# Layer 0's entry: x tiles loaded and normed behind the context tiles' projection

## Chip, cores, metric

One core of a Trainium2 chip. The metric is the device time of one execution in microseconds (us). The engines are TensorE (PE: matmuls and transposes), VectorE (DVE), ScalarE (ACT), GpSimd (POOL) and SyncE (SP, which here issues nearly all DMA transfers). Each runs its own instructions in the order in which they were put on its queue; across engines they wait for each other by semaphores.

## The reference

A two-layer backbone: 512 latent tokens `x` and 256 context tokens `ctx`, width 1024. Each layer makes a modulation (shift, scale, gate) from a conditioning vector, one for x tokens and one for context tokens, and applies it behind an RMS norm. Layer 0 then projects to queries, keys and values and attends; what matters here is its beginning:

```python
s_c = jax.nn.silu(c)
s_cc = jax.nn.silu(c_ctx)[None, :]
mx = (s_c @ mod_w[l] + mod_b[l])[:, None, :]
mc = (s_cc @ mod_w[l] + mod_b[l])[:, None, :]
shx1, scx1, gx1, shx2, scx2, gx2 = jnp.split(mx, 6, axis=-1)
shc1, scc1, gc1, shc2, scc2, gc2 = jnp.split(mc, 6, axis=-1)
hx = _rms(x, norm_mix_w[l]) * (1.0 + scx1) + shx1
hc = _rms(ctx, norm_mix_w[l]) * (1.0 + scc1) + shc1
ax, ac = _even_mixer(hx, hc, ev_w_in[i], ev_w_out[i], ...)   # projections hx @ w_in, hc @ w_in, heads, attention
```

## The kernel before

Tokens lie in six tiles of 128: tiles 0 to 3 are x, tiles 4 and 5 are context. Projections run over them in the order `CTX_FIRST = (4, 5, 0, 1, 2, 3)`. Activations are held transposed (`hT` for x, `hTc` for context: 128 partitions, 8 column blocks k, tokens), each as two numbers: `hi`, rounded by a cast on ACT, and `lo`, the remainder by a subtraction on DVE or POOL. Weights are split the same way (`wih` L330, `wil` L331). A product takes three matmuls per k: hi x hi, hi x lo, lo x hi (`project`, L428 to L430).

The order of instructions is made by a scheduler at build time: it simulates the engines and puts on each queue, among the instructions that are ready, the one that comes first in the program, if no priority or edge says otherwise. `tc.issue_after(ins)` adds such an edge: what is traced inside it on `ins`'s engine goes behind `ins`.

The entry of layer 0 does this:

- SP loads the context tiles, then modulation weights for shift and scale (parts 0 and 1, four chunks each, two pieces of 512 KB per chunk, `modw`, L177). Fourteen of the sixteen pieces and block 0's four weight units use six buffers (`start_tile`, tag `mw`) in turn; two pieces use the two buffers of `raw_tile` (tag `raw`). A buffer is loaded again only when what read it is done.
- The four x tiles (`load_x`, L337) are loaded in the middle of this, after the first two pairs of chunks in the program.
- All six tiles are normed together (loop at L912): Square on ACT (L914), `rsqrt` on POOL (L158, L159), the product on DVE (L915), eight transposes per tile on PE (L919), copies to a transposed buffer `xT` on ACT (L920).
- Once a column block's modulation is known (`modc`, `aff`, L241, L245), DVE scales it for context and for x (L925), ACT casts it to `hi` (L930), and DVE (x) or POOL (context) makes `lo` (L931).
- Then block 0's projection weights (`weights0`: four units of 256 rows, three DMAs each, L326), the rope tables (`tables0`: `rp` in a `raw` buffer, read by four DVE products `rt`, L350 and L352), and the projections of block 0 (`in_proj0`), each followed by the norm and rotation of the heads on ACT, DVE and POOL, and by transposes of the previous tile's heads (`late`, L491, L497).
- Blocks 1 to 3 load their weights into `raw` buffers and make `lo` on POOL; the attention of block b runs beside the projection of block b + 1.

Of the kernel before, what the change touches and what calls it, by code (L numbers as in the profile page):

```python
# [10 lines left out]
F32 = mybir.dt.float32  # L11
F32R = mybir.dt.float32r
BF16 = mybir.dt.bfloat16
AF = mybir.ActivationFunctionType
ALU = mybir.AluOpType
# [3 lines left out]
P = 128  # L19
D = 1024  # L20
KT = D // P
SEQ = 512
CTX = 256
NT = (SEQ + CTX) // P
NTX = SEQ // P
TOK = SEQ + CTX
# [7 lines left out]
CTX_FIRST = (4, 5, 0, 1, 2, 3)  # L34
# [29 lines left out]
def backbone(es: ExitStack, tc: tile.TileContext, x, c, ctx, c_ctx, mod_w, mod_b, norm_mix_w, norm_ffn_w,  # L64
# [3 lines left out]
    nc = tc.nc  # L68
# [4 lines left out]
    small = es.enter_context(tc.tile_pool(name="small", bufs=6))  # L73
# [1 line left out]
    dram = es.enter_context(tc.tile_pool(name="dram", bufs=1, space=bass.MemoryType.DRAM))  # L75
    p_1 = es.enter_context(tc.tile_pool(name="p_1", bufs=1, space=PSUM))
    turn = {"acc": 0, "tr": 0, "sum": 0}
    marks = {}

    def mark(ins):  # L80
        marks[ins.ins.engine] = ins.ins
# [19 lines left out]
    def raw_tile(shape, name):  # L101
        return keep.tile(shape, F32, name=name, tag="raw", bufs=2)
# [7 lines left out]
    def tr_tile(name, shape, dt=F32, one=None):  # L110
        if one is None:
            one = turn["tr"] = 1 - turn["tr"]
        return p_1.tile(shape, dt, name=name, tag=f"tr{one}")

    def f32(ap):
        return ap.bitcast(F32)
# [4 lines left out]
    start = Pool("start")  # L121
# [7 lines left out]
    ident = cst[:, C_ID:C_ID + P]  # L129
# [25 lines left out]
    def rsqrt(ss, n, inv, tag):  # L155

        r = small.tile([P, n], F32, name="rs_" + tag, tag="rs_" + tag)
        nc.gpsimd.tensor_scalar(r, ss, inv, EPS, ALU.mult, ALU.add)  # L158
        nc.gpsimd.tensor_tensor(r, r, neghalf[:, :n], ALU.pow)  # L159
        return r  # L160
# [3 lines left out]
    modc = [cp.tile([P, 6, KT, 2], F32, name=f"modc{l}") for l in range(2)]  # L164
    aff = [cp.tile([P, 2, KT, 2], F32, name=f"aff{l}") for l in range(2)]
# [108 lines left out]
    def cols_T(j, s0, s1):  # L274

        return hT[j][0][:, :, s0:s1] if s1 <= SEQ else hT[j][1][:, :, s0 - SEQ:s1 - SEQ]
# [45 lines left out]
    def unit(pool, views, shape, bufs, name, sub=None, new_tile=raw_tile):  # L322

        raw = new_tile(shape, name + "r")
        for dst, src in views(raw):
            nc.sync.dma_start(dst, src)  # L326
        p_hi, p_lo = pool if isinstance(pool, tuple) else (pool, pool)
        hi = p_hi.tile(shape, F32R, name=name + "h", tag="whi", bufs=bufs)
        lo = p_lo.tile(shape, F32R, name=name + "l", tag="wlo", bufs=bufs)
        nc.scalar.copy(hi, raw)  # L330
        (sub or nc.vector.tensor_sub)(lo, raw, f32(hi))  # L331
        return hi, lo

    def load_x(t, back=False):
        xt = keep.tile([P, D], F32, name=f"x{t}", tag="xo", bufs=6)
        src, t0 = (out if back else x, t) if t < NTX else (ctx, t - NTX)
        nc.sync.dma_start(xt, src[0, t0 * P:(t0 + 1) * P, :])  # L337
        return xt
# [83 lines left out]
    def project(ps, t, ws, c0, c1):  # L422

        hs = [tile_T(j, t) for j in range(2)]
        for k in range(KT):
            whi, wlo = ws[k // 2]
            a, b = whi[:, k % 2, c0:c1], wlo[:, k % 2, c0:c1]
            nc.tensor.matmul(ps, hs[0][:, k, :], a, start=k == 0, stop=False)  # L428
            nc.tensor.matmul(ps, hs[0][:, k, :], b, start=False, stop=False)  # L429
            nc.tensor.matmul(ps, hs[1][:, k, :], a, start=False, stop=k == KT - 1)  # L430

    def residual(xt, ps, g, n, pool=None, eng=nc.vector, rb=2):

# [12 lines left out]
    def weights0(b, wp, sub, new_tile=raw_tile):  # L446

        qc, kc, vc = ((b * 256, 512 + 64 * b, 640 + 64 * b) if b < 2 else
                      (768 + (b - 2) * 256, 1280 + 64 * (b - 2), 1408 + 64 * (b - 2)))
        ws = []  # L450
        for u in range(4):
            def views(raw, u=u):
                for c0, c1, s in ((0, 256, qc), (256, 320, kc), (320, 384, vc)):
                    yield raw[:, :, c0:c1], ev_w_in[0, u * 256:(u + 1) * 256, s:s + c1 - c0].rearrange(
                        "(j p) n -> p j n", p=P)
            ws.append(unit(wp, views, [P, 2, 384], WBUF, "wi", sub, new_tile))
        return ws
# [4 lines left out]
    def in_proj0(b, ws, tabs, wp, st, qp):  # L462

        wc, tb = tabs[b // 2]
        kT = st.tile([P, 2, TOK], F32R, name="kT", tag="kT")
        vv = st.tile([P, NT, HD], F32, name="vv", tag="vv")
        qs = {}
        late = None
        yield qs, kT, vv
        for t in CTX_FIRST:  # L470
            ps = acc_tile("inps", 384, one=0) if b else p_sc.tile([P, 1024], F32, name="inps", tag="sc")[:, :384]
            project(ps, t, ws, 0, 384)
            raw = wp.tile([P, 384], F32, name="qkv", tag="qkv", bufs=2)
            nc.scalar.copy(raw, ps)
            nc.gpsimd.tensor_copy(vv[:, t, :], raw[:, 320:384])
            y, r = rotate(raw[:, 0:320], 4, 1, t, wc, tb, wp)
            nc.gpsimd.tensor_tensor(y, y, bc(r, 2, HD), ALU.mult)
            qd = wp.tile([P, 4, 2, HD], F32R, name="qd", tag="qd", bufs=2)
            nc.scalar.copy(qd[:, :, 0, :], y[:, 0:4])
            nc.vector.tensor_sub(qd[:, :, 1, :], y[:, 0:4], f32(qd[:, :, 0, :]))  # L480
            kd = wp.tile([P, 2, 2, HD], F32R, name="kd", tag="kd", bufs=2)
            kb = bc(y[:, 4, :], 1, 2)
            mark(nc.scalar.copy(kd[:, 0], kb))
            mark(nc.gpsimd.tensor_sub(kd[:, 1], kb, f32(kd[:, 0])))
            if late:
                late()

            def late(t=t, qd=qd, kd=kd):
                pt = tr_tile("qpt", [P, 4, P], F32R)
                for h in range(4):  # L490
                    nc.tensor.transpose(pt[:, h, :], qd[:, h].rearrange("p a d -> p (a d)"), identr)  # L491
                qt = qp.tile([P, 4, P], F32R, name="qt", tag="qt", bufs=6)
                nc.scalar.copy(qt, f32(pt))
                qs[t] = qt
                pk = tr_tile("kpt", [P, 2, P], F32R)
                for j in range(2):
                    nc.tensor.transpose(pk[:, j, :], kd[:, j].rearrange("p a d -> p (a d)"), identr)  # L497
                nc.scalar.copy(kT[:, :, t * P:(t + 1) * P], f32(pk))
            if t == CTX_FIRST[-1]:
                late()  # L500
            yield

    def attend0(b, t, state, o_t, sink, negsink, mp):

# [401 lines left out]
    xs = {t: load_x(t) for t in CTX_FIRST[:2]}  # L906
    start_mod(0)
    start_mod(1)
    xs.update({t: load_x(t) for t in CTX_FIRST[2:]})
    xT = start.pool.tile([P, KT, TOK], F32, name="xT")  # L910
    for t in CTX_FIRST:
        h = start.pool.tile([P, D], F32, name="nh", tag="nh", bufs=2)  # L912
        ss = small.tile([P, 1], F32, name="nss", tag="nss")
        nc.scalar.activation(h, xs[t], AF.Square, accum_out=ss)  # L914
        nc.vector.tensor_scalar(h, xs[t], rsqrt(ss, 1, 1.0 / D, "n"), None, ALU.mult)  # L915
        for g in range(2):
            pt = tr_tile("npt", [P, 4, P])
            for k in range(4):
                nc.tensor.transpose(pt[:, k, :], h[:, (4 * g + k) * P:(4 * g + k + 1) * P], ident)  # L919
            nc.scalar.copy(xT[:, 4 * g:4 * g + 4, t * P:(t + 1) * P], pt)  # L920
    start_mod(2)
    start_mod(3)
    for k in range(KT):
        for i, (s0, s1) in ((1, (SEQ, TOK)), (0, (0, SEQ))):
            nc.vector.tensor_scalar(xT[:, k, s0:s1], xT[:, k, s0:s1], aff[0][:, 0, k, i:i + 1],  # L925
                                    modc[0][:, 0, k, i:i + 1], ALU.mult, ALU.add)
        for s0, s1, ks in ((SEQ, TOK, slice(k - 1, k + 1)), (0, SEQ, slice(k, k + 1))):
            if s0 == 0 or k % 2:
                hi, lo = (cols_T(j, s0, s1)[:, ks, :] for j in range(2))
                nc.scalar.copy(hi, xT[:, ks, s0:s1])  # L930
                (nc.gpsimd if s0 else nc.vector).tensor_sub(lo, xT[:, ks, s0:s1], f32(hi))  # L931


    mods = [(0, part, n) for part in (2, 3, 4) for n in range(4)]
    ws = weights0(0, wp.pool, None, start_tile)
    tabs = {}
    tables0(0, tabs, wp.pool)

# [8 lines left out]
    even = Pool("even0")  # L947
    proj = in_proj0(0, ws, tabs, wq.pool, even.pool, wq.pool)
    state = next(proj)
    for _ in proj:  # L950
        pass
    o_t = [keep.tile([P, KT, P], F32, name=f"o{t}", tag="xo", bufs=6) for t in range(NT)]
    att = Pairs()
    for b in range(4):
        order = CTX_FIRST if b < 3 else tuple(range(NT))
        att.push(attend0(b, order[0], state, o_t, sink, negsink, at.pool))
        proj = None
        if b < 3:
            if b == 1:
                tables0(1, tabs, wp.pool)  # L960
            ws = weights0(b + 1, wp.pool, nc.gpsimd.tensor_sub)
            proj = in_proj0(b + 1, ws, tabs, wq.pool, (even if b % 2 else odd).pool, (wq if b % 2 else odd).pool)
            nxt = next(proj)
        if b == 3:
# [4 lines left out]
            ws = [Pool("w0u", "right"), Pool("w0d", "right")]  # L969
# [200 lines left out]
```

## Time and profile before

| what | value |
|---|---|
| runs | 1807.63, 1807.75, 1808.97 us; median 1807.75 |
| profiled execution | 1810.42 us, span 1808.6 us |
| mean granted TensorE clock | 0.985 |
| busy in the span: PE / DVE / ACT / POOL | 95% / 56% / 45% / 33% |
| busy in the first 44 us: PE / DVE / ACT / POOL | 26.13 / 19.20 / 26.83 / 9.25 us |
| DMA in the first 44 us | share 0.97, 315 GB/s |

The span is the time from the first to the last instruction of the profiled execution; its own time lies 1.8 us above it. Shares are means over stages with different limits, so the first 75 us are read by themselves. In a list of instructions each row has start, duration, engine, line and operation, the tile written and those read, and in brackets how long the engine stood idle before it and what ended that.

### The profile page before, as it was taken

To read this page: it belongs to the slowest core of one execution; us is meant where nothing else is said; L and a number is where in the kernel's file an instruction comes from. 1 tells how busy PE (TensorE), PEld (TensorE's weight loads), DVE (VectorE), ACT (ScalarE), POOL (GpSimd) and SP (SyncE) were. 2 spreads that over 40 slices of the span, in tenths; PEclk is the share of its full clock that TensorE was granted. 3 is DMA by queue.
4 is the path that set the end of the run, shared out by engine and by line. 5 is a ranking of instruction groups with operands and counts; after the bars stand their busy time and mean duration, and the time that the engine had idled before them with its cause. 6 is when DMAs were issued, how large, how long until landed. Compare 5 with 4: busy or idle time off the path is not lost. (4 is left out here: it accounts for less than half of the span.)

```text
span 1808.6 us, 26168 instructions
## 1 busy us (share of the span) xinstructions
PE 1725.4 (95%) x9958; PEld 1462.3 (81%) x9958; DVE 1005.0 (56%) x1737; ACT 809.2 (45%) x1710; POOL 601.7 (33%) x866
## 2 busy tenths in 40 slices
PE   6999999989999999999999989999988899999998
PEld 3887776767888888888888889999986788888887
DVE  4776465444365555555543656665674455656553
ACT  6566555433354344344332566665663432222220
POOL 2753333321064344233312567776643100000000
PEclk8999999999999999999999999999989999999999
DMA  9212233213543234344421111111122233233231
GB/s 313 53 42 92 74 103 120 70 36 105 163 152 105 82 105 140 116 140 128 128 85 40 63 36 50 47 45 36 33 71 82 73 110 109 70 105 105 70 107 56
DMA packets 152477, 165.64 MB, mean 92 GB/s; under 512 B 16480, under 2 KB 139936, under 8 KB 152352
## 3 DMA queue, kind: packets, MB, share of 16 engines
q1 hardware_dynamic: 152000, 163.77, 28.7%
q8 instruction: 78, 1.28, 0.3%
q14 instruction: 47, 0.39, 0.1%
q10 hardware_dynamic: 352, 0.21, 0.0%
HBM read 159.73 MB, written 4.22 MB: 91 GB/s over the span
## 5 line engine op out<-in xcount | busy, mean ns | idle before, releaser
L435 DVE TENSOR_TENSOR dps<-dps,g 128x512 f32<-128x512 f32 x200 | 136.0, 695 | 108.5 <-PE dps L848 100.2
L846 PE MATMUL dps<-wdh,hdh 128*128 128x512 f32 x440 | 176.0, 401 | 0.9 <-DVE x L436 0.9
L847 PE MATMUL dps<-wdl,hdh 128*128 128x512 f32 x440 | 174.3, 396 | 0.0
L848 PE MATMUL dps<-wdh,hdl 128*128 128x512 f32 x440 | 168.1, 396 | 0.0
L428 PE MATMUL inps<-wih,hT 128*128 128x384 f32 x384 | 134.1, 349 | 2.3 <-ACT qkv L626 2.3
L436 DVE TENSOR_TENSOR x<-x,dps 128x512 f32<-128x512 f32 x200 | 131.9, 680 | 2.8
L429 PE MATMUL inps<-wil,hT 128*128 128x384 f32 x384 | 131.9, 343 | 0.0
L430 PE MATMUL inps<-wih,hT 128*128 128x384 f32 x384 | 131.4, 342 | 0.0
L791 PE MATMUL pg<-hT,wgh 128*128 128x512 f32 x352 | 129.8, 392 | 0.0
L791 PE MATMUL pu<-hT,wuh 128*128 128x512 f32 x352 | 129.4, 391 | 0.3 <-DVE x L436 0.3
L212 ACT ACTIVATE modw<-modw,cols 128x256 f32<-128x256 f32 x192 | 82.3, 498 | 81.7 <-DMA modw<-in_mod_w_dram 75.1
L791 PE MATMUL pgu<-hT,wgh 128*128 128x512 f32 (+1 forms) x384 | 114.2, 381 | 3.8 <-DVE x L436 2.9
L791 PE MATMUL pgu<-hT,wuh 128*128 128x512 f32 (+1 forms) x384 | 113.7, 376 | 0.0
L791 PE MATMUL pg<-hTc,wgh 128*128 128x256 f32 x352 | 98.7, 284 | 2.7 <-ACT hTc L307 2.4
L846 PEld LDWEIGHTS dps<-wdh,hdh 128*128 128x128 f32 x440 | 82.7, 188 | 22.5 <-issue 3.3
L791 PE MATMUL pu<-hTc,wuh 128*128 128x256 f32 x352 | 98.8, 285 | 0.0
L848 PEld LDWEIGHTS dps<-wdh,hdl 128*128 128x128 f32 x440 | 82.3, 188 | 19.7
L330 ACT CAST wgh<-wgr 128x1024 fp32r<-128x1024 f32 x44 | 46.1, 1049 | 116.0 <-PE pgu L791 69.5
L847 PEld LDWEIGHTS dps<-wdl,hdh 128*128 128x128 f32 x440 | 82.8, 188 | 17.9
L331 DVE TENSOR_TENSOR wgl<-wgr,wgh 128x1024 fp32r<-128x1024 f32 x44 | 54.3, 1236 | 75.5 <-ACT wgh L330 75.5
L320 POOL TENSOR_TENSOR wil<-wir,wih 128x256 fp32r<-128x256 f32 x96 | 76.4, 825 | 57.9 <-ACT wih L330 57.7
L331 DVE TENSOR_TENSOR wul<-wur,wuh 128x1024 fp32r<-128x1024 f32 x44 | 58.2, 1322 | 61.6 <-ACT wuh L330 61.6
(258 smaller groups left out, 4633.0 us busy)
## 6 DMA issues: line engine op xcount, KB each, us to landing
modw<-in_mod_w_dram SPq DMA_DIRECT2D x96, 512.0 KB, 4.5
wgr<-in_ffn_w_in_dram SPq DMA_DIRECT2D x44, 512.0 KB, 3.5
wur<-in_ffn_w_in_dram SPq DMA_DIRECT2D x44, 512.0 KB, 3.5
wdr<-in_ffn_w_out_dram SPq DMA_DIRECT2D x44, 512.0 KB, 3.6
wir<-in_od_w_in_dram SPq DMA_DIRECT2D x96, 128.0 KB, 2.3
x<-in_x_dram SPq DMA_DIRECT2D x8, 512.0 KB, 4.8
wir<-in_ev_w_in_dram SPq DMA_DIRECT2D x16, 256.0 KB, 2.9
wor<-in_ev_w_out_dram SPq DMA_DIRECT2D x8, 512.0 KB, 3.6
```

The source lines that it names most:

```text
L212: nc.scalar.activation(pr[:, k], w[:, k], AF.Copy, scale=cols[:, kk:kk + 1])
L320: nc.gpsimd.tensor_sub(lo[c], raw[c], hi[c])
L331: (sub or nc.vector.tensor_sub)(lo, raw, f32(hi))
L428: nc.tensor.matmul(ps, hs[0][:, k, :], a, start=k == 0, stop=False)
L429: nc.tensor.matmul(ps, hs[0][:, k, :], b, start=False, stop=False)
L430: nc.tensor.matmul(ps, hs[1][:, k, :], a, start=False, stop=k == KT - 1)
L435: nc.vector.tensor_mul(tmp, ps, g[:, n * 512:(n + 1) * 512])
L436: eng.tensor_add(xt[:, n * 512:(n + 1) * 512], xt[:, n * 512:(n + 1) * 512], tmp)
L791: nc.tensor.matmul(ps[:, s0:s1], a, cols_T(b, s0, s1)[:, k, :], start=k == 0 and q == 0, stop=k == KT - 1 and q == 2)
L846: nc.tensor.matmul(ps, hh, a, start=j == 0, stop=False)
L847: nc.tensor.matmul(ps, hh, b, start=False, stop=False)
L848: nc.tensor.matmul(ps, hl, a, start=False, stop=j == nj - 1)
```

## The change

- The x tiles are loaded behind block 0's last weight load on SP's queue (`loaded["unit"]`, `issue_after`) instead of between modulation pieces.
- The loop of norms at the entry covers the two context tiles only; `xT` holds context columns only. Their `lo` is made on POOL for the first three pairs of columns and on DVE for the last.
- x is normed in two pairs by a new function `start_pair`, traced after the first and the second projected context tile; its transposes go behind that tile's last matmul on PE. The norm's product moves from DVE to POOL and is made in place; Square and the scaled columns use the two `raw` buffers; scaling reads the transposes in PSUM, on DVE and ACT in turn; casts are on ACT and subtractions on DVE, in four chunks per pair.

```diff
-            nc.sync.dma_start(dst, src)
+            loaded["unit"] = nc.sync.dma_start(dst, src).ins
...
-            nc.tensor.matmul(ps, hs[1][:, k, :], a, start=False, stop=k == KT - 1)
+            last = nc.tensor.matmul(ps, hs[1][:, k, :], a, start=False, stop=k == KT - 1)
+        return last.ins
...
-            project(ps, t, ws, 0, 384)
+            done = project(ps, t, ws, 0, 384)
...
-            yield
+            yield done
...
-    xs.update({t: load_x(t) for t in CTX_FIRST[2:]})
-    xT = start.pool.tile([P, KT, TOK], F32, name="xT")
-    for t in CTX_FIRST:
+    xT = start.pool.tile([P, KT, CTX], F32, name="xT")
+    for t in CTX_FIRST[:2]:
...
     for k in range(KT):
-        for i, (s0, s1) in ((1, (SEQ, TOK)), (0, (0, SEQ))):
-            nc.vector.tensor_scalar(xT[:, k, s0:s1], xT[:, k, s0:s1], aff[0][:, 0, k, i:i + 1],
-                                    modc[0][:, 0, k, i:i + 1], ALU.mult, ALU.add)
-        for s0, s1, ks in ((SEQ, TOK, slice(k - 1, k + 1)), (0, SEQ, slice(k, k + 1))):
-            if s0 == 0 or k % 2:
-                hi, lo = (cols_T(j, s0, s1)[:, ks, :] for j in range(2))
-                nc.scalar.copy(hi, xT[:, ks, s0:s1])
-                (nc.gpsimd if s0 else nc.vector).tensor_sub(lo, xT[:, ks, s0:s1], f32(hi))
+        nc.vector.tensor_scalar(xT[:, k], xT[:, k], aff[0][:, 0, k, 1:2], modc[0][:, 0, k, 1:2], ALU.mult, ALU.add)
+        if k % 2:
+            ks = slice(k - 1, k + 1)
+            hi, lo = (cols_T(j, SEQ, TOK)[:, ks, :] for j in range(2))
+            nc.scalar.copy(hi, xT[:, ks])
+            (nc.gpsimd if k < 6 else nc.vector).tensor_sub(lo, xT[:, ks], f32(hi))
+
+    def start_pair(t0):
+        for t in (t0, t0 + 1):
+            ss = small.tile([P, 1], F32, name="nss", tag="nss")
+            nc.scalar.activation(raw_tile([P, D], "sq"), xs[t], AF.Square, accum_out=ss)
+            nc.gpsimd.tensor_scalar(xs[t], xs[t], rsqrt(ss, 1, 1.0 / D, "n"), 1.0, ALU.mult, ALU.mult)
+        hi, lo = (cols_T(j, t0 * P, (t0 + 2) * P) for j in range(2))
+        for g in range(2):
+            hc = raw_tile([P, 4, 2 * P], "nhc")
+            for k0 in (0, 2):
+                pt = tr_tile("npt", [P, 2, 2 * P])
+                for k in range(2):
+                    kk = 4 * g + k0 + k
+                    for i in range(2):
+                        nc.tensor.transpose(pt[:, k, i * P:(i + 1) * P], xs[t0 + i][:, kk * P:(kk + 1) * P], ident)
+                for k in range(2):
+                    kk = 4 * g + k0 + k
+                    a, c = aff[0][:, 0, kk, 0:1], modc[0][:, 0, kk, 0:1]
+                    if k:
+                        nc.scalar.activation(hc[:, k0 + k, :], pt[:, k, :], AF.Identity, bias=c, scale=a)
+                    else:
+                        nc.vector.tensor_scalar(hc[:, k0 + k, :], pt[:, k, :], a, c, ALU.mult, ALU.add)
+                ks = slice(4 * g + k0, 4 * g + k0 + 2)
+                nc.scalar.copy(hi[:, ks], hc[:, k0:k0 + 2])
+                nc.vector.tensor_sub(lo[:, ks], hc[:, k0:k0 + 2], f32(hi[:, ks]))
...
     ws = weights0(0, wp.pool, None, start_tile)
+    with tc.issue_after(loaded["unit"]):
+        xs.update({t: load_x(t) for t in CTX_FIRST[2:]})
     tabs = {}
     tables0(0, tabs, wp.pool)
...
-    for _ in proj:
-        pass
+    for i, done in enumerate(proj):
+        if i < 2:
+            with tc.issue_after(done):
+                start_pair(2 * i)
```

More of the change, by code (lines that the diff above doesn't have):

```diff
@@ L77, in backbone @@
     turn = {"acc": 0, "tr": 0, "sum": 0}
-    marks = {}
+    marks, loaded = {}, {}
     def mark(ins):
@@ L919, in backbone @@
                 nc.tensor.transpose(pt[:, k, :], h[:, (4 * g + k) * P:(4 * g + k + 1) * P], ident)
-            nc.scalar.copy(xT[:, 4 * g:4 * g + 4, t * P:(t + 1) * P], pt)
+            nc.scalar.copy(xT[:, 4 * g:4 * g + 4, (t - NTX) * P:(t - NTX + 1) * P], pt)
     start_mod(2)
```

## The prediction

> **What bounds the kernel now.** I read the page first, then the start of the span in windows, then its order of time, then the tiles that the change touches.
>
> ```profile
> span 1808.6 us, 26168 instructions
> PE 1725.4 (95%) x9958; PEld 1462.3 (81%) x9958; DVE 1005.0 (56%) x1737; ACT 809.2 (45%) x1710; POOL 601.7 (33%) x866
> PE   6999999989999999999999989999988899999998
> ```
>
> TensorE (PE) is busy 95% of the span and only the first slice is poor. So whatever brings steady matmul work forward in the first 60 us is kept to the end, unless another engine gives it back.
>
> ```profile
> 2.00:14.00 12.00, 3.40 (x23) 2.08 (x24) 2.15 (x5) 6.22 (x11) 1.95 (x4) 1.00 1.05 339
> 16.00:20.00 4.00, 2.65 (x28) 1.36 (x25) 1.25 (x6) 3.28 (x7) 0.63 (x2) 1.00 1.02 419
> 20.00:36.00 16.00, 12.83 (x84) 8.47 (x84) 7.61 (x16) 9.57 (x19) 3.75 (x8) 0.57 0.98 329
> ...
> 40.00:46.00 6.00, 4.02 (x21) 3.15 (x20) 5.96 (x14) 4.60 (x8) 1.60 (x1) 1.00 0.79 201
> 41.00:55.80 14.80, 10.81 (x56) 9.28 (x55) 13.82 (x24) 7.79 (x13) 6.96 (x4) 1.00 0.47 125
> 55.80:100.00 44.20, 42.92 (x280) 41.33 (x280) 32.38 (x79) 28.17 (x78) 37.29 (x60) 1.00 0.17 44
> ```
>
> The columns are stretch, length, busy time of PE, its weight loads, DVE, ACT, POOL, then clock, DMA share, GB/s. Up to 36 us the DMA engines are full (share about 1). From 41 to 55.8 DVE is: 13.82 of 14.8 us, while the DMA share falls to 0.47. From 55.8 on PE is, 42.92 of 44.2, with POOL next at 37.29. So the entry has two limits in turn, loads and then DVE; the order of time shows the second.
>
> ```profile
> 38.78 1.07 PE L183 MATMUL mod<-modw,s_pad 128*32 128x256 f32 x16
> ...
> 43.25 1.57 ACT L330 CAST wih<-wir 128x768 fp32r<-128x768 f32 x2
> ...
> 46.86 0.15 DVE L245 SCALAR_TENSOR_TENSOR aff<-modc,cols 128x4 f32<-128x4 f32 x1
> ...
> 49.14 3.14 DVE L925 TENSOR_SCALAR xT<-xT,aff,modc 128x256 f32<-128x256 f32 x4
> ...
> 52.06 0.61 ACT L930 CAST hTc<-xT 128x512 fp32r<-128x512 f32 x1
> ...
> 52.75 1.31 POOL L931 TENSOR_TENSOR hTc<-xT,hTc 128x512 fp32r<-128x512 f32 x1 [1.85 <-ACT hTc L930]
> ...
> 54.12 0.44 PE L430 MATMUL inps<-wih,hTc 128*128 128x384 f32 x1 [0.42 <-POOL hTc L931]
> ...
> 55.81 0.34 PE L428 MATMUL inps<-wih,hT 128*128 128x384 f32 x1
> ...
> 73.96 0.34 PE L430 MATMUL inps<-wih,hT 128*128 128x384 f32 x1
> 74.13 0.34 PE L429 MATMUL inps<-wil,hTc 128*128 128x384 f32 x1
> ```
>
> The last modulation matmuls start at 38.78, but their scale (aff) is formed only at 46.86, since DVE splits weights and scales x tiles in between; the last context columns follow at 52.06, and x tile 0 starts at 55.81. The four x tiles take 55.81 to 74.3, 18.5 us, at 0.17 us per matmul (the last two rows); block 1's projection follows directly.
>
> **The change part by part.**
>
> *Loads.* Four x loads leave the place behind the sixth modulation piece and go behind the weights.
>
> ```profile
> modw<-in_mod_w_dram SPq DMA_DIRECT2D x16, 512.0 KB, 7.7
> x<-in_x_dram SPq DMA_DIRECT2D x4, 512.0 KB, 8.8
> ```
>
> Four times 512 KB is 2.1 MB, at 419 GB/s 5.0 us. All modulation and block 0's weights come 5.0 us earlier: last modulation matmul 38.78 to about 33.8, the last weight units, cast from 43.25 on, landed by about 39. On SP the x issues now stand behind twelve weight issues and in front of the rope table (rp), which shares two raw buffers with the new squares. Bytes ahead of rp are the same as before, so its data, still lands near 43.5 (my estimate: before, it went last in the stretch 40 to 46, which moved 1.2 MB and ran empty before its end; its products there waited for DVE, not for it).
>
> *Context.* DVE loses eight 512-wide scalings and eight 512-wide subtractions from this place and four of six norm products. With aff no longer queued behind them, the context tiles' last columns are ready near 37, the last weight unit split near 41, and the 48 context matmuls (48 x 0.17 = 8.2 us) can end near 43 instead of 55.8. That is 12 us, but the x tiles are not ready then.
>
> *The x pairs.* Two tiles go through Square (ACT), rsqrt and product (POOL), transposes (PE), scaling (DVE and ACT in turn), cast and subtraction. The nearest rows are the later norms of the same form:
>
> ```profile
> L298 PEld LDWEIGHTS npt<-cst,nh x72: 138/140/143, 412.6 to 1026.7; 128*128 128x128 f32 x72
> ...
> L290 ACT ACTIVATE nh<-x x9: 1046/1060/1063, 406.0 to 1016.3; 128x1024 f32<-128x1024 f32 x9
> L290 ACT ACTIVATION_READ_ACCUMULATOR nh<-x x9: 184/186/188, 407.0 to 1017.3; 128x1 f32 x9
> L292 POOL TENSOR_SCALAR nh<-x,rs_n x9: 1122/1125/1564, 408.2 to 1019.6; 128x1024 f32<-128x1024 f32 x9
> ```
> ```profile
> L303 ACT ACTIVATE nhc<-npt,modc,aff x36: 440/457/461, 413.9 to 1028.8; 128x128 f32<-128x128 f32 x36
> L307 ACT CAST hT<-nhc x10: 607/618/627, 415.6 to 1029.7; 128x512 fp32r<-128x512 f32 x10
> L308 DVE TENSOR_TENSOR hT<-nhc,hT x10: 679/692/1434, 416.3 to 1030.4; 128x512 fp32r<-128x512 f32 x10
> ```
> ```profile
> L350 DVE TENSOR_TENSOR rt<-rp,rw x2: 412/412/413, 46.9 to 47.6; 128x256 f32<-128x256 f32 x2
> ```
> ```profile
> L159 POOL TENSOR_TENSOR rs_n<-rs_n,neghalf 128x1 f32<-128x1 f32 x6 | 3.3, 554 | 0.5
> ...
> L158 POOL TENSOR_SCALAR rs_n<-nss 128x1 f32<-128x1 f32 x6 | 1.8, 294 | 20.1 <-ACT nh L914 20.1
> ```
> ```profile
> SPq L326 <- DVE rt L352: 4.3, 1, 4.3
> ```
>
> The last row shows what the two raw buffers do: already now a weight load stood 4.3 us on the SP queue until the rope products had read rp. In the changed kernel the second Square takes that buffer. So x tile 1 is not gated by its own load but by rp: 43.5, four products (two in the row above, two like them) 4 x 0.41 = 1.65, Square and its read 1.25, rsqrt 0.85, product 1.13, four transposes about 0.8 with their drain, a 256-wide scaling about 0.5 (estimate between 0.46 at 128 and 0.62 at 512 columns), cast 0.62: 6.8 us, and seven handovers at 0.07 (52.06 + 0.61 to 52.75 and 52.75 + 1.31 to 54.12 above: 0.08 and 0.06), 7.3 in all. Tile 0 can start at 50.8, not 55.81: 5.0 us sooner.
>
> Four chunks of a pair follow each other at ACT's 0.5 + 0.62 = 1.1 us, as fast as PE uses them. The second pair's squares wait for the first pair's chunk buffers (the later one free at 50.8 + 3 x 1.1 + 0.69 = 54.8), and the same chain without rp, 5.2 us and its handovers, puts its first columns at about 60.4; tiles 0 and 1 keep PE until 50.8 + 9.25 = 60.1 (half of 18.5). It arrives just in time. Its 16 transposes now stand in a full PE: 16 x 0.14 = 2.2 us; the first pair's lie in the gap between 43 and 50.8. The x stage ends at 50.8 + 18.5 + 2.2 = 71.5 instead of 74.3: 2.8 us, and up to 1.6 more if the context heads' transposes also find the gap. I take 3.0.
>
> *What comes back.* All four weight units of block 1 now queue behind the second pair in the raw buffers; before, two were split by 55.
>
> ```profile
> L326 SPq DMA_DIRECT2D wir<-in_ev_w_in_dram x24: 367/461/479, 33.7 to 57.3; - x24
> L330 ACT CAST wih<-wir x6: 827/832/838, 39.6 to 53.4; 128x768 fp32r<-128x768 f32 x6
> ...
> DMA to landing us min/median/max: 2.9/3.5/4.9
> ```
> ```profile
> 74.66 1.84 POOL L331 TENSOR_TENSOR wil<-wir,wih 128x768 fp32r<-128x768 f32 x1
> ```
>
> Each unit takes about 2 x 0.46 + 3.5 to land, 0.83 for the cast and 1.84 for the subtraction: 7.1 us, two at a time. With the buffers free at about 62.3 and 64.6, the fourth ends at 64.6 + 2 x 7.1 = 78.8, where 74.66 + 1.84 = 76.5 is the time before, and PE would want it 3 us sooner than that. PE has block 0's context attention to do meanwhile. The loss is between 0 (all filled) and 5.3 us (78.8 against 73.5). The nearest row is the stretch 55.8 to 100, where PE lost 1.3 us in all though POOL was busy 84%; I take 0.8, a good half of it again. POOL gets four rsqrts and products, 7.9 us, most of it before 58; its share after that rises and is why I do not take 0.
>
> Sum: -3.0 + 0.8 = -2.2 us. The profiled execution took 1810.42 us around its 1808.6 span, 2.7 above the median of the three runs; taken from the median 1807.75 that gives 1805.5. About 0.2%, 3.6 us, is what a measurement here can tell from no change.
>
> **Rivals.**
>
> *rp is no gate (clearly faster).* If rp's load is put ahead of x, or its products are done when x 1 lands, tile 0 starts at x 1's landing, 39 plus half of the 5.0 us, 41.5, plus 5.6 for the chain, 47. Then the x stage ends at 47 + 20.7 = 67.7, 6.6 us sooner, and the buffers come free 3.8 earlier; with a few tenths given back, 1801.4 (1799 to 1803.5). Against it: the order of the code puts rp behind x, and the loads in front of it are ready to issue when its buffer comes free.
>
> *The weights of block 1 come late (slower).* One mechanism, the two raw buffers. If the second pair ends 6 us later than I have it (rotations of the context tiles stand in front of it on POOL, which then has 7.9 us more), the fourth unit is split at 85. PE then has done block 0's context attention and can only wait: 85 against 76.5 before is 8.5, less about 4 us of other work done ahead: +4 to +5, 1812. It decides from the point where the fourth unit is later than about 81. For it: POOL at 37.29 of 44.2 after 55.8. Against: the order is written so that each tile's norm comes before the later rotations.
>
> *The clock.*
>
> ```profile
> 18.00:20.00 2.00, 0.65 (x4) 0.20 (x2) 1.25 (x6) 1.95 (x4) 0.63 (x2) 1.00 1.03 421
> 20.00:22.00 2.00, 0.96 (x5) 0.99 (x6) 1.35 (x4) 1.01 (x3) 1.44 (x4) 0.71 1.06 379
> ...
> 32.00:34.00 2.00, 2.00 (x24) 0.79 (x16) 1.29 (x2) 0.95 (x3) 0.00 (x0) 0.50 0.50 128
> 34.00:36.00 2.00, 2.00 (x28) 0.83 (x20) 0.98 (x5) 0.37 (x1) 0.00 (x0) 0.88 1.06 367
> ```
>
> After a stretch with PE busy 0.65 of 2 us the granted clock fell to half, and came back only after PE had been fully busy from 32 on at the latest, some 3 us. The new gap from 43 to 50.8 holds only transposes. If it halves the clock, tiles 0 and 1 lose half of some 4 us, the two full stretches shown: +2, 1807.5.
> The Trainium skill, page "TensorE: Matmul & The Clock Gate", Part 1, says that one idle window of about 3.4 us throttles TensorE to half and one busy window of the same length restores it; by its figure the loss would be an estimated 1.7 us instead of 2. The fall and return above agree with the rule in kind; that it speaks against a gap in the middle of the projections is why this case has a chance of its own.
>
> *The loads do not come sooner.* Modulation pieces past the sixth need a buffer that a modulation matmul frees; if that paces them, x only filled the hole and nothing is won: 1808. Against it: the DMA share is about 1 up to 36 us also where no x was under way.
>
> **How the numbers follow.** Forecast as summed, -0.5 to -3.6 and a little past it: 0.42. rp no gate: 0.32. Clock or loads, together 0.10, within 0.2%. Late weights: 0.16. Faster by over 0.2% is 0.32 and 0.04 of the forecast's fast edge, 0.36; slower 0.17 (0.01 from the clock); the rest, 0.47, is no change. The range takes in the fast rival nearly whole and half of the slow one: 1799.5 to 1811.5; the forecast alone 1804 to 1807.3.
>
> **What the changed profile would show.** Last modulation matmuls near 34; aff within 4 us of them; context matmuls ending near 43; rope products right before the second x Square near 45; first x matmul near 51; two transposing groups of 16 in the projections; block 1's four weight splits all after 62. Wrong if the first x matmul is before 48 (fast rival), if block 1's last split is past 81 (slow rival), if the granted clock is half at 51, or if the modulation matmuls have not moved.

## The result, and the profile after

The changed kernel is slower: median 1822.27 us (1816.67 to 1825.08, four runs) against 1808.36 us of the kernel before on the same chip (1807.63 to 1809.37, four runs), ratio 1.0073 with an interval of 1.0046 to 1.0099, some 13 us. Its profiled execution took 1824.06 us, 13.6 above that of the kernel before.

The page after (length, busy time of the engines, PE by fortieths) hides it: the share of PE is 95% as before.

```profile
span 1822.2 us, 26160 instructions
PE 1734.8 (95%) x9958; PEld 1470.1 (81%) x9958; DVE 988.7 (54%) x1734; ACT 809.6 (44%) x1710; POOL 610.5 (34%) x869
PE   6899999989999999999999989999988899999999
```

The first question is how far into the program the loss has arisen. The rows of the product of probabilities and values in layer 1's attention give two marks, first and last start. Before:

```profile
L695 PE MATMUL av<-vv,PT x384: 271/275/421, 1083.7 to 1411.5; 128*128 128x128 f32 x192
```

After:

```profile
L696 PE MATMUL av<-vv,PT x384: 270/275/421, 1098.1 to 1425.9; 128*128 128x128 f32 x192
```

The first is 14.4 us late, and between the two marks both kernels take 327.8 us. So the loss is there before layer 1's attention and does not grow in it. The stretch 36 to 100 us in windows (columns as in the prediction), before:

```profile
36.00:100.00 64.00, 57.29 (x374) 52.26 (x374) 51.05 (x114) 39.42 (x97) 45.52 (x64) 1.00 0.31 80
```

Of it, the two parts that matter below:

```profile
78.00:82.10 4.10, 2.82 (x16) 2.28 (x15) 3.43 (x11) 3.31 (x11) 3.78 (x8) 1.00 0.30 84
82.10:92.30 10.20, 10.20 (x73) 10.05 (x73) 7.13 (x17) 7.16 (x24) 9.37 (x16) 1.00 0.21 48
```

After, the whole stretch and its parts:

```profile
36.00:100.00 64.00, 53.87 (x296) 49.93 (x295) 40.33 (x99) 41.02 (x96) 44.13 (x63) 0.87 0.25 77
...
34.00:44.00 10.00, 10.00 (x70) 9.06 (x58) 7.36 (x16) 7.29 (x14) 4.23 (x7) 0.98 0.85 287
...
44.00:48.00 4.00, 1.14 (x9) 0.67 (x7) 4.00 (x12) 1.45 (x4) 3.76 (x6) 1.00 0.00 0
48.00:54.80 6.80, 6.34 (x22) 5.85 (x23) 4.70 (x9) 6.59 (x15) 4.61 (x9) 0.50 0.00 0
...
78.00:82.10 4.10, 1.45 (x6) 0.91 (x6) 4.10 (x13) 2.85 (x4) 3.31 (x5) 1.00 0.35 96
82.10:92.30 10.20, 7.84 (x28) 6.93 (x29) 5.66 (x14) 5.60 (x20) 7.06 (x13) 0.50 0.22 65
```

PE has 296 matmuls recorded instead of 374; 32 of the difference are modulation matmuls, which now lie ahead of 36 us. From 34 to 44 PE is busy 10.00 us, where the kernel before had 7.25: the front works. Then come two holes, at 44 and at 78, each followed by a stretch at half clock. The DMA share is 0.00 from 44 to 54.8 us: nothing is loaded there, although block 1's weights are wanted next.

In order of time, the rows that decide it:

```profile
33.37 1.51 PE L183 MATMUL mod<-modw,s_pad 128*32 128x256 f32 x16
...
41.16 1.06 ACT L935 ACTIVATE sq<-x 128x1024 f32<-128x1024 f32 x1
...
45.73 0.45 DVE L350 TENSOR_TENSOR rt<-rp,rw 128x256 f32<-128x256 f32 x1
...
47.19 0.53 DVE L952 TENSOR_SCALAR nhc<-npt,aff,modc 128x256 f32<-128x256 f32 x1
...
56.97 1.13 POOL L936 TENSOR_SCALAR x<-x,rs_n 128x1024 f32<-128x1024 f32 x1
...
61.59 0.93 PE L945 MATMUL npt<-cst,x 128*128 128x128 f32 x7
63.77 0.66 PE L945 MATMUL npt<-cst,x 128*128 128x128 f32 x4 [1.25 <-ACT nhc L950]
64.64 0.44 PE L428 MATMUL inps<-wih,hT 128*128 128x384 f32 x1 [0.21 <-ACT hT L954]
...
70.59 0.80 DVE L955 TENSOR_TENSOR hT<-nhc,hT 128x512 fp32r<-128x512 f32 x1 [0.75 <-ACT hT L954]
72.19 1.85 POOL L331 TENSOR_TENSOR wil<-wir,wih 128x768 fp32r<-128x768 f32 x1 [1.34 <-ACT wih L330]
...
84.97 1.82 POOL L331 TENSOR_TENSOR wil<-wir,wih 128x768 fp32r<-128x768 f32 x1 [0.67 <-ACT wih L330]
```

And SP's DMA queue, first its order of time, then its waits between 36 and 100 us (total, times, longest):

```profile
67.42 11.85 SPq L326 DMA_DIRECT2D wir<-in_ev_w_in_dram  x12
```
```profile
SPq L326 <- DVE hT L955: 29.2, 1, 29.2
```

The rope products and the head work stand in front of the first x scaling at 47.19; the second pair's rows are normed at 58.1, but PE gets to seven of their first eight transposes only at 61.59, behind tiles 0 and 1 (one runs at 60.08); tile 2 starts at 64.64. And SP's next weight load waits 29.2 us, in one piece, for a subtraction: the one that reads the first of the second pair's two chunk buffers (66.67 to 67.35). The other comes free with the subtraction at 70.59. Block 1's four units are split from 72.19 to 86.79 us. Before, the first two of them were early, and the fourth ended at 76.50:

```profile
48.30 2.59 POOL L331 TENSOR_TENSOR wil<-wir,wih 128x768 fp32r<-128x768 f32 x1 [3.80 <-ACT wih L330]
54.36 1.96 POOL L331 TENSOR_TENSOR wil<-wir,wih 128x768 fp32r<-128x768 f32 x1 [0.29 <-ACT wih L330]
```

The x stage itself ends at 75.19 us, 0.9 later than before. The next stage shows the loss: the projection of block 1's first context tile is copied out 11.8 us late, here first before, then after:

```profile
79.89 0.47 ACT L474 COPY qkv<-inps 128x384 f32<-128x384 f32 x1
```
```profile
91.73 0.48 ACT L475 COPY qkv<-inps 128x384 f32<-128x384 f32 x1 [0.54 <-PE inps L430]
```

In between lies the second hole. PE's own wait there (after, 36 to 100 us) is for the softmax (`Pt`) of the first attention tile:

```profile
PE sc L535 <- ACT Pt L549: 4.6, 2, 4.1
```

It stands from 79.45 to 83.55. The projection of that context tile could not go on before 82.87 either, when the third weight split ended, so the late weights alone would have held it for 3.4 of the 4.1 us. A third, smaller hole comes later. From 150 to 160 us PE is busy 7.99 us (10.00 before), and from 160 to 170 the clock is 0.83:

```profile
159.41 1.07 PE L183 MATMUL mod<-modw,s_pad 128*32 128x256 f32 x16 [2.01 <-DMA modw<-in_mod_w_dram]
```

### The profile page after: what moved, and what is told of

Read it like the earlier page. It is cut to its first block, busy times and chain, and to the rows that moved or that the text cites. A ratio compares the mean times of both kernels' runs of the same rounds, so it can differ in the third digit from the quotient of the medians.

```text
span 1822.2 us, 26160 instructions
## 1 busy us (share of the span) xinstructions
PE 1734.8 (95%) x9958; PEld 1470.1 (81%) x9958; DVE 988.7 (54%) x1734; ACT 809.6 (44%) x1710; POOL 610.5 (34%) x869
```

## The experiments

The two theories at the start. *Buffers*: block 1's weights are held by the two raw buffers until the second pair is through them, and PE runs out of work. *Clock*: the hole at 44 us halves the clock, and everything after comes late. Ratios are to the kernel before on the same chip.

**Fill the first hole** (24 unread matmuls of 128x384 behind the last context tile's projection; the function `fill`, which issues them, is left out here):

```diff
     for i, done in enumerate(proj):
+        if i == 1:
+            fill(24, ws[0][0], done)
```

> The changed kernel with 24 extra 128x384 matmuls (their result is never read) queued on TensorE behind the second context tile, in the gap of 43.0 to 49.6 us. Theory 'clock': the two stretches at half clock after TensorE's gaps (48.0 to 54.8 and 82.1 to 92.3 in the changed kernel's trace) are most of the loss; with the first gap filled the clock stays 1.00 from 48 to 55, the x stage ends about 3.4 us earlier and the time falls to about 1818. Rival 'late supply': the end of the x stage is set by the second pair's chain and what follows by block 1's weights; the clock stays up but the time stays within 1.5 us of 1822.

1816.93 us, ratio 1.0058 (1.0041 to 1.0075). The clock is whole there (its window), and tile 2 starts at 64.12 instead of 64.64 (its order of time):

```profile
48.00:54.80 6.80, 5.43 (x35) 4.64 (x35) 4.71 (x11) 5.31 (x13) 3.63 (x6) 1.00 0.00 0
```
```profile
63.47 0.66 PE L953 MATMUL npt<-cst,x 128*128 128x128 f32 x4 [1.54 <-ACT nhc L958]
64.12 0.44 PE L428 MATMUL inps<-wih,hT 128*128 128x384 f32 x1
```

With the whole clock PE stood idle for 1.4 of the 6.8 us, and the x stage ends where it did (75.12, 75.19 without the filler). The filler also put off the first x matmul, from 49.57 to 51.68 us, so this run does not price the half clock by itself. The time is what 'clock' forecast, but it did not come about as that theory says: the heads of block 1's first context tile are still 10.4 us late (11.8 without the filler), and most of the gain arises at the third hole, which is missing here (PE busy 9.83 us from 150 to 160). The loss stays; the intervals with and without the filler overlap.

**Fill both holes** (24 more behind the second head's scores of the first attention tile):

> As before, and 24 more such matmuls behind the second head's scores of the first attention tile, in the gap of 79.5 to 83.5 us. 'Clock': no half clock from 36 to 160 us, time about 1813 (3.4 + 5.1 us less). 'Late supply': the matmuls that wait for weights and scores end when they did; time 1820 or more.

1817.38 us, ratio 1.0057 (1.0042 to 1.0072). The clock is whole in the second place too:

```profile
82.00:92.30 10.30, 8.28 (x53) 7.59 (x52) 6.55 (x15) 6.80 (x21) 8.70 (x14) 1.00 0.24 66
```

With the clock whole in both places the loss is still 10 us. The filler's own time, up to 24 x 0.17 = 4.1 us in the second place, may hide a gain of that size. The half clock is thus not shown to cost nothing, but some 6 of the 13 us at least are not its doing.

**x loaded early again, all else as changed**:

```diff
     start_mod(1)
+    xs.update({t: load_x(t) for t in CTX_FIRST[2:]})
...
-    with tc.issue_after(loaded["unit"]):
-        xs.update({t: load_x(t) for t in CTX_FIRST[2:]})
```

> One part undone: the x loads go back between the modulation pieces, all else as changed. 'Clock': context projection ends about 5 us later (48), but the first pair is normed by then, so there is no gap before tile 0, no half clock at 48 to 55; time 1814 to 1818. Theory 'the load move is the gain': tile 0 starts later than 52 and the time is 1822 or more.

1819.0 us, ratio 1.0073 (1.0057 to 1.0089), the changed kernel's own. Tile 0 starts at 54.58 us, 5 later than with the loads moved, and the end does not notice: a start that is 5 us sooner was worth nothing here. The clock is 1.00 from 44 to 54.8 us in this run, without any filler, and the loss is the same; block 1's last split ends at 88.79 us, even later than in the changed kernel.

**Chunk buffers of their own** (`nhc` leaves the raw buffers for the six buffers that later hold the attention's output):

```diff
-            hc = raw_tile([P, 4, 2 * P], "nhc")
+            hc = keep.tile([P, 4, 2 * P], F32, name="nhc", tag="xo", bufs=6)
```

> The scaled columns of the pairs use buffers of the x tiles' ring instead of the two raw buffers, so block 1's weight loads need not wait for the second pair. 'Late supply': block 1's four splits end by 76 instead of 86.8, the gap at 79.5 to 83.5 closes and with it the half clock at 82 to 92; time 1811 to 1815. 'Clock' with the first gap as the cause: block 1's splits earlier, but the first half-clock stretch stays and the time falls by at most 5 us, to 1817 or more.

1812.66 us, ratio 1.0029 (1.0016 to 1.0041). This line gives back 0.0044 x 1807 = 8 of the 13 us. The weights' load starts at 45.54 instead of 67.42. SP no longer waits for the pairs' subtractions; a wait of 7.8 us ahead of the load is left, which the profile puts down to ACT and which ends as the last of the pairs' Squares does (45.51), since the Squares still use the raw buffers (waits of SP from 36 to 100 us, then order of time):

```profile
SPq L326 <- POOL wil L331: 16.3, 5, 6.6
SPq L343 <- POOL wil L331: 13.8, 1, 13.8
SPq L326 <- ACT sq L402: 7.8, 1, 7.8
```
```profile
45.54 14.86 SPq L326 DMA_DIRECT2D wir<-in_ev_w_in_dram  x12
...
54.18 2.32 POOL L331 TENSOR_TENSOR wil<-wir,wih 128x768 fp32r<-128x768 f32 x1
```

The fourth split ends at 77.19, and from 78 to 82.1 us PE is busy 3.71 of 4.1 us. x tile 2 starts at 67.29, later still than in the changed kernel.

**Both pairs behind the first context tile, buffers of their own**:

```diff
-        if i < 2:
+        if i == 0:
             with tc.issue_after(done):
-                start_pair(2 * i)
+                start_pair(0)
+                start_pair(2)
```

> The own-buffers kernel with both pairs traced behind the first context tile, so the second pair's norm and transposes come ahead of the second context tile's later work. Theory 'second pair's chain sets the end of the x stage': x tile 2 starts by 62 instead of 67, and the time falls below the own-buffers kernel's 1812.7, to 1807 to 1810. Rival 'only block 1's weights count': the same 1812 to 1814.

1808.10 us, ratio 0.9999 (0.999 to 1.0009), ten runs: the rest of the loss, 0.003 x 1808 = 5 us, is gone as well. The second pair's first columns are transposed at 54.86 instead of 62.49 with the pair behind the second tile, and x tile 2 starts at 62.97 instead of 67.29.

**The same order with the raw buffers**, which completes the square:

> The changed kernel with both pairs traced behind the first context tile, the chunk buffers still the two raw ones (the order alone, without buffers of its own). Buffers are the main cause: block 1's four weight units still stand behind the second pair, which only comes some 5 us sooner; last split at about 82 instead of 86.8, ratio to before about 1.004, 1814 to 1817. Order is the main cause (the second pair behind the rotations): the loss goes nearly whole, ratio 1.001 or less, whatever the splits show.

1823.75 us, ratio 1.0090 (1.0073 to 1.0107): in the total the order alone gives back nothing. The second pair's Squares, at 42.08 and 44.58 with buffers of its own, are at 52.46 and 53.97 here, because they too need a raw buffer, and SP waits as in the changed kernel:

```profile
SPq L326 <- DVE hT L955: 29.8, 2, 28.3
```

| ratio to before | raw buffers | buffers of their own |
|---|---|---|
| second pair behind the second tile | 1.0073 | 1.0029 |
| both pairs behind the first tile | 1.0090 | 0.9999 |

This last kernel was slower than both theories had it. Part of that is not from the entry at all: the marks of layer 1's attention, and PE's wait for weight splits there (1100 to 1400 us), in this kernel:

```profile
L696 PE MATMUL av<-vv,PT x384: 270/275/421, 1089.0 to 1423.7; 128*128 128x128 f32 x192
```
```profile
PE inps L429 <- POOL wil L320: 5.8, 3, 2.0
```

It is 334.7 us from mark to mark instead of 327.8. The scheduler writes the order of the whole program from its own simulation, and the orders of these kernels differ down to layer 1. Between the marks, three of the thirteen traces share one order of operations that no other has: this one, the next one and the one with the rope tables first. They take 334.4 to 335.5 us there, the other ten 325.3 to 329.9. So 6.9 us are lost here at a place that the edit does not touch. Ahead of it the order does help: the first mark is at 1089.0, 9.1 us sooner than in the changed kernel. Less the 6.9 us the ratio would be about 1.0052, an estimate. With it in the table, buffers of their own are worth 8 to 10 us in both rows, and the order 4 to 5 us in both columns.

**Late weights put into the kernel before** (two tiny raw tiles written only behind x tile 2's projection; nothing else changed):

```diff
             nc.scalar.copy(raw, ps)
+            if b == 0 and t == 2:
+                for _ in range(2):
+                    nc.scalar.copy(raw_tile([P, 8], "hold"), raw[:, :8])
```

> The kernel before with one suspected cost added: two tiny tiles hold the two raw buffers until x tile 2's head values are copied (about 70 us), so block 1's four weight units load only then, as in the changed kernel; nothing else changes. 'Late supply': block 1's splits at 74 to 84, a gap of TensorE near 78 to 82 with half clock after it, time 5 to 9 us above before. 'Late weights do not matter': within 2 us of before.

1825.97 us, ratio 1.0101 (1.0087 to 1.0114). SP stands 27.5 us on the held buffers, the DMA engines are idle from 50 to 68, and the load starts at 70.92 (waits of SP, a window, the mark):

```profile
SPq L326 <- ACT hold L477: 27.5, 1, 27.5
```
```profile
50.00:68.00 18.00, 16.20 (x85) 15.84 (x86) 10.57 (x27) 7.95 (x19) 11.21 (x18) 0.91 0.00 0
```
```profile
L698 PE MATMUL av<-vv,PT x384: 270/275/421, 1092.1 to 1426.5; 128*128 128x128 f32 x192
```

By the marks 8.4 us are lost ahead of layer 1's attention (1092.1 against 1083.7) and 6.6 in it (334.4 against 327.8 us), where PE again waits for weight splits, 7.9 us in all. By the runs the loss is 0.0101 x 1808 = 18 us, which leaves some 12 without the 6.6. The x stage ends at 74.32 us as before, and the heads of block 1's first context tile are copied 13.4 us late (93.26 against 79.89). So a delay of block 1's weights, without anything else of the change in the code, costs 8 to 12 us at the place in question, at least as much as the line with the buffers gave back; the other part is again the scheduler's order further on.

**Own buffers and the first hole filled**:

> Own buffers and the 24 extra matmuls in the first gap together. If the half clock behind the first gap and the late weights cost separately, the two gains add (-5 and -9.6 from 1822): about 1808. If both act through the same thing (late work after 75 us), no further gain: 1811 to 1814.

1813.0 us, ratio 1.0034 (1.0023 to 1.0045): with the buffers free the filler gains nothing. **Both pairs early, own buffers, both holes filled**:

> Both pairs behind the first context tile, chunk buffers of their own, and unread matmuls in the two gaps (24 of 128x384 behind the last context tile's projection, 24 behind the second head's scores of the first attention tile). If the half clock (48 to 53 and 86 to 92 in the kernel without the filler, some 3.4 us of full-speed work) is all that keeps this version from being faster than before, the ratio falls to 0.9985, about 1805. If supply by the other engines sets these places, the filler changes nothing or costs its own time: 1.000 to 1.002.

1814.34 us, ratio 1.0042 (1.0028 to 1.0057): it costs 0.0043 x 1807 = 8 us over the same kernel without it. The first 24 matmuls put off the first x matmul, from 50.20 to 51.83 us, and the other 24 take up to 4.1 us. The clock is whole from 36 to 100 us in it, and that gained nothing that shows.

Two tries at a faster version. **The kernel before, with its x tiles scaled, cast and subtracted only behind the first context tile** (loads, norms and transposes as before):

> One part alone, on the kernel before: x is loaded, normed and transposed where it was (early), but its scaling, casts and subtractions are traced behind the first projected context tile, so that DVE serves the context first; the raw buffers are left to the weights as before. Theory 'order of DVE work is the good part, raw buffers and late pairs the bad one': context projection ends near 47, tile 0 follows at 47 to 49 without a gap, block 1's splits stay where they were (two by 56), x stage ends by 70; time 4 to 6 us below the kernel before. Rival 'moving any x work behind the context brings the heads late': no gain, within 2 us of before.

1808.87 us, ratio 1.0008 (0.9999 to 1.0017): no change. The edit did not do what it was for: the heads of the second context tile are copied at 56.6 us (56.0 before), where the projection was to end near 47, and tile 0 starts at 56.38. So this run does not test what an earlier context is worth. **Both pairs early, own buffers, and the rope tables loaded ahead of block 0's weights**:

```diff
+    tabs = {}
+    tables0(0, tabs, wp.pool)
     ws = weights0(0, wp.pool, None, start_tile)
```

> Both pairs behind the first context tile, chunk buffers of their own, and the rope tables loaded ahead of block 0's weights, so that their four products on VectorE (1.7 us at 45.9 to 47.4 in the kernel with both pairs behind the first tile) leave the place ahead of the first x scaling. First x matmul counts: it starts at 48 to 49 instead of 50.2, the x stage ends 1 to 2 us sooner and the time falls by as much, 0.9990 of before, 1806. The x stage's start is not what the end hangs on (as with the filler and the earlier x loads): ratio 1.000 within 0.001, or slower by the rope's bytes ahead of the weights.

1817.42 us, ratio 1.0052 (1.0034 to 1.007). The rope products are out of the way (40.0 us), but the first x matmul starts at 50.97, not sooner than 50.20 without this edit; POOL's product, which the transposes wait for, ends at 47.17 there instead of 45.57. The x stage still ends 1.1 us sooner (72.93 against 73.99). Layer 1's attention takes 335.5 us, with 5.9 of waits for weight splits:

```profile
L696 PE MATMUL av<-vv,PT x384: 270/275/421, 1080.6 to 1416.1; 128*128 128x128 f32 x192
```
```profile
PE inps L429 <- POOL wil L320: 5.9, 3, 2.0
```

The first mark is 3.1 us sooner than before, and 7.7 are lost between the marks. The 3.1 are no gain that is shown: this profiled execution was 1.8 us faster than the median of its runs, and that of the kernel before 2.7 slower than its own. No version beat the kernel before.

## Why the prediction was wrong

*Loads: right.* The last modulation matmuls are at 33.37 (33.8 was forecast), the x loads are issued at 34.85.

*Context: right.* The last of its matmuls starts at 43.71, where an end near 43 was forecast.

*rp as the gate of x tile 1: wrong.* Its Square ran at 41.16, four us before the rope products, so its scratch tile did not wait for rp's buffer. That the first x matmul came at 49.57, near the 50.8 forecast, is luck: other things set it. On POOL the product of tile 1 started only at 43.92 and took 1.44 us; on DVE the rotation of the first context heads and the rope products (43.90 to 47.19) stand in front of the first scaling, whose transposes were done by 46.3; on ACT a cast of heads (48.40) stands in front of the chunk's cast. I had counted what each step takes and what its buffer waits for, but not these queues at that moment. No one of them is shown to be the gate: with the rope products moved away, the first x matmul came no sooner (50.97). So the fast rival, "rp is no gate", whose condition held, did not get its 47.

*The second pair "just in time": wrong, and the first of the two steps that decided.* Forecast were first columns at 60.4 and an x stage ending at 71.5. The product was done at 58.1, near enough; the transposes then stood behind tiles 0 and 1 on PE, 61.59, tile 2 started at 64.64, and block 1's projection at 75.15 (74.13 before). I charged the 16 transposes as PE time in a full PE, 2.2 us, but not as a chain that can only start when PE's queue lets it. The -3.0 us were +1: the x stage ended at 75.19 instead of 74.3. Tiles 0 and 1 held PE for 12.0 us (49.57 to 61.59) instead of the 9.25 forecast, at half clock from 48 to 54.8; what share of the delay that is, no run separates. Run with both pairs early and own buffers, where the chain is out of the way, this part is worth 5 us.

*"What comes back": mis-sized, and the main error.* The mechanism, two raw buffers holding block 1's four weight units behind the second pair, was in the sum, at 0.8 us between bounds of 0 and 5.3. The buffers came free at 67.35 and 71.39 (62.3 and 64.6 were forecast), the fourth split ended at 86.79 (78.8), and what the square of runs gives for it is 8 us, up to 10 by the estimate there. I took 0.8 because the stretch 55.8 to 100 of the kernel before lost only 1.3 us. But that stretch had two units split early, at 48.30 and 54.36; with none before 72 there is nothing of block 1 to fill PE with while the first attention tile waits for its softmax. A stretch that shows no loss shows what its cover is worth, not what its loss would be.

*The slow rival* was thus the right case, and its threshold fits: it decides from about 81 us for the fourth unit, and that came at 86.79. Its price, +4 to +5, failed in the deduction of "about 4 us of other work done ahead": from 78 to 82.1 us PE was busy 1.45 of 4.1 us, then at half clock. And its chance, 0.16, rested on "each tile's norm comes before the later rotations", which the traces do not bear out for PE and DVE.

*The clock rival:* the half clock came, at 48 as feared, and again at 82.1. Its price of 2 us fits what can be read: from its first matmul to its end the x stage took 25.6 us, and 23.4 with the first hole filled. But the filler itself cost 2.1 us at the start, so the stage's end stayed where it was, and the loss of 13 us is not this rival's.

*What stays open:* how much of the remaining time the half clock at 82 to 92 us takes by itself, between 0 and about 4 us; how the scheduler comes to the order of layer 1 that costs three of the kernels 6 to 8 us; how the third hole, at 159 us, hangs together with the rest; and why the version with the loss removed, whose first x matmul is 5.6 us sooner than before, ends level. When the heads of block 1's second context tile are copied, 2.8 us of its lead are left (82.94 against 85.71). From 82.1 to 92.3 us PE is then busy 8.67 us at a mean clock of 0.83, where the kernel before had 10.20 at 1.00, which is about 3 us of work (an estimate). Whether that half clock or what PE waited for is the cause, no run separates: the filler that was to do so cost time itself.

## What to carry to other kernels

Before new scratch tiles go into a small ring of buffers, list who else draws from that ring and when its next user must start loading: the DMA queue's longest single wait, here 29.2 us on a subtraction of another stage, shows it in one row. An earlier start of a stage is worth only what the last of its parts gains; price each later part as a chain that must pass the queues of the engines that the earlier parts now fill. Where a scheduler orders the whole program, compare marks in parts that the edit does not touch before crediting the edit with the difference.

## What was not expected of the hardware

The half clock outlasts the hole. After 4.0 us with PE busy 1.14 it was half for 6.8 us, although PE was busy 6.34 of these; the second time it lasted 10.2 us. The clock changes at 48.0, 54.8, 82.1 and 92.3 us, and the distances (6.8, 27.3 and 10.2) are 2, 8 and 3 times 3.4 us. Cut at these points into stretches of 3.4 us, the changed kernel's trace reads:

| stretch, us | PE busy, us | clock in it |
|---|---|---|
| 44.6 to 48.0 | 0.87 | 1.00 |
| 48.0 to 51.4 | 2.94 | 0.50 |
| 51.4 to 54.8 | 3.40 | 0.50 |
| 54.8 to 58.2 | 3.40 | 1.00 |
| 78.7 to 82.1 | 0.75 | 1.00 |
| 82.1 to 85.5 | 1.96 | 0.50 |
| 85.5 to 88.9 | 2.80 | 0.50 |
| 88.9 to 92.3 | 3.08 | 0.50 |

The clock is half behind a stretch with PE busy 0.87 or 0.75 us, stays so behind 1.96, 2.80 and 2.94, and is whole again behind 3.08 and 3.40. So one stretch that is nearly full is enough here; the half clock lasted for two and three because the ones before had waits in them. In the thirteen traces, cut in the same way from 20 to 1800 us, each of the 118 falls stands behind a stretch with PE busy at most 2.30 us, and each of the 131 returns behind one with at least 2.73. The Trainium skill, page "TensorE: Matmul & The Clock Gate", Part 1, gives a window of about 3.4 us after which it falls when idle and returns when busy. These rows agree with it, and show that the window before a fall need not be wholly idle.

Small DVE operations beside a POOL split of 128x768 take as long as that:

```profile
76.00 1.84 POOL L331 TENSOR_TENSOR wil<-wir,wih 128x768 fp32r<-128x768 f32 x1 [1.55 <-ACT wih L330]
76.34 1.79 DVE L418 TENSOR_TENSOR qy<-qkv,rt 128x256 f32<-128x256 f32 x1 [4.60 <-ACT qkv L475]
...
81.08 1.79 POOL L331 TENSOR_TENSOR wil<-wir,wih 128x768 fp32r<-128x768 f32 x1
81.14 1.75 DVE L545 SCALAR_TENSOR_TENSOR nm<-mx,negsink 128x1 f32<-128x1 f32 x1
...
83.21 0.36 DVE L545 SCALAR_TENSOR_TENSOR nm<-mx,negsink 128x1 f32<-128x1 f32 x1
```

The 128x1 operation takes 1.75 us, where the median of its 48 rows in this trace is 0.15, and both DVE rows end close to the POOL row beside them (78.13 and 77.84; 82.89 and 82.87). The Trainium skill, page "GPSIMD Engine Reference", section 1, says that GpSimd shares its SBUF interfaces with VectorE and contends with VectorE instructions that have two SBUF inputs; these rows agree. So late weight splits do not only come late: at 81 us one ran beside an operation on the chain of the softmax for which PE waited 4.1 us, and ACT waited 1.59 us for it.
